# A 64-row second product for the attention scores, run over 128 rows with q low loaded twice

## The chip, the cores and the metric

The kernel runs on one core of one Trainium2 chip. The metric is the device time of one execution in microseconds (us); the median of three runs stands for a kernel. One further execution is recorded by the hardware profiler; its rows are what is read below. Engines: PE is TensorE's matmul side and PEld its weight load, DVE is VectorE, ACT ScalarE, POOL GpSimd, SP the queue that issues the DMAs.

## What is computed

One layer of a streaming encoder over 1072 token rows (32 sample rows, 16 learned meta rows, 1024 prompt rows): a mixer of three head groups (forgetting attention, multi-scale pooling, a chunked state-space scan), an output projection, and a dense gated FFN. The change touches the attention alone, six heads of 64:

```
s = einsum('bqhd,bkhd->bhqk', q, k) * HD_FOX ** -0.5
s = s + c_q[..., :, None] - c_k[..., None, :]          # cumulative log-forget bias
p = softmax(where(k_pos <= q_pos, s, -inf))
out = einsum('bhqk,bkhd->bqhd', p, v)
```

The prompt part is causal over 1040 rows; the 32 sample rows see 256 cached keys and their own.

## The kernel before, in words

All arithmetic is float32 to the outside. For TensorE every operand is split into a high part that the fast float32 format holds exactly and a low part, the rest; a product of two split operands is then three passes (high by high, high by low, low by high). `mm` (line 69) records every such product, so that nearly all of them carry line 69 and are told apart by the tile they write.

The program runs in stages: the input projection and the scan (to about 240 us), the attention (240 to 472 us), the output projection with its norms (to about 560 us) and the FFN (the rest). In the attention stage the order on each engine is written out by hand: the `while` loop of line 1124 runs in ticks. A tick issues, where they are due, one chunk of scores (`s_products`, line 995), one group of transposes of finished exponentials (`t_turn`, tiles `t`), the products with v (`o_products`, tiles `o`), the vector and scalar work that belongs to earlier ticks, and then filler: products of the next projections (`wk`) while there are any, later those of the output projection's first part (`wp`). How much filler follows is worked out from a planner's clock with a fixed estimate of TensorE's time (2 products by their columns, 100 ns on top, line 1141), and a head's scores are issued once the planner's clock has passed the estimated arrival of its loads (line 1138).

A head's operands lie in one tile `H`, of which there are two (`HA`, `HB`), filled by `prep(h)` (line 839) with DMAs from copies in HBM: K has k high in partitions 0 to 63 and k low in 64 to 127, Q has q high twice, QL has q low in partitions 0 to 63, bc the bias row, V and Vm the values. `arrival` (line 475) adds each DMA's bytes to the planner's estimate.

A chunk of scores takes up to 512 keys for up to 128 queries. It is one accumulation of two or three products: q high twice by K over 128 rows (which is high by high plus high by low in one pass), a mask product `identr` by `am` on the diagonal, and last q low by k high over 64 rows (line 1019). DVE then adds the bias and finds the row minimum (line 1029), ACT exponentiates (line 1040), PE transposes. There are 15 chunks in a head: four of 512 keys without a mask; one of 16, 144, 272, 400 or 512 keys with a mask two times each; and one of 304 keys for the 48 first queries, whose mask product has 48 rows. Six heads make 90 chunks.

Of the kernel before, what the change touches and what calls it, by code (L numbers as in the profile page):

```python
# [15 lines left out]
P = 128  # L16
D = 1024
NK = 8
NT = 1072
# [3 lines left out]
KEYS = PAST + NT  # L23
# [27 lines left out]
def tile_hybrid_trunk(ctx: ExitStack, tc: tile.TileContext, a: dict):  # L51
# [16 lines left out]
    def mm(out, lhsT, rhs, start, stop):  # L68
        return nc.tensor.matmul(out, lhsT, rhs, start=start, stop=stop, skip_group_check=True)  # L69
# [28 lines left out]
    def psum(tag, name):  # L98
        return where.get(tag, psp[0]).tile([P, 512], F32, tag=tag, bufs=PSB[tag], name=name)
# [14 lines left out]
    qd = [dr.tile([2, P, NT], F32, name=f"qd{p}") for p in range(3)]  # L114
# [7 lines left out]
    cd = dr.tile([6, KEYS], F32, name="cd")  # L122
# [110 lines left out]
    for t in range(9):  # L233
        R, o = TROW[t], TOFF[t]
# [4 lines left out]
        ps = zps[t]  # L239
# [98 lines left out]
    def cv_tile(tag, name):  # L338
        return CV.tile([P, EW], F32, tag=tag, bufs={"ext": 2, "cv": 4}[tag], name=name)
# [53 lines left out]
    for b in range(3):  # L393
        c0, n = CH[b]
        ps = psum("sm", f"ft{b}")
        for t in CTILES[b]:
            R, c = TROW[t], TOFF[t] - c0
# [47 lines left out]
    for i in range(5):  # L445
# [9 lines left out]
        h = cv_tile("cv", f"ch{i}")[:, :W]  # L455
# [19 lines left out]
    def arrival(nbytes):  # L475
        queue[0] = max(queue[0], clock[0]) + nbytes / 330.0
        return queue[0] + LATE[0]
# [333 lines left out]
    live, n = [], 0  # L811
# [27 lines left out]
    def prep(h):  # L839
        pr, hb = h // 2, 64 * (h % 2)  # L840
        H = (HB if h % 2 else HA).tile([P, HW], F32R, tag="H", name=f"H{h}")

        K, Q, QL = H[:, :KEYS], H[:, KEYS:KEYS + NT], H[:64, KEYS + NT:KEYS + 2 * NT]
        bc = H[:, KEYS + 2 * NT:2 * KEYS + 2 * NT]
        V = H[:, 2 * KEYS + 2 * NT:HW - P].rearrange("p (t c) -> p t c", c=P)
        Vm = H[:, HW - P:]
        heads[h] = (Q, QL, K, V, Vm, bc)
        v = vd[pr][:, h % 2].rearrange("r d j -> r (d j)")
        hs = slice(hb, hb + 64)
        loads = [(K[:64], kd[pr][0, hs]), (Q[:64], qd[pr][0, hs]), (K[64:], kd[pr][1, hs]), (Q[64:], qd[pr][0, hs]),  # L850
                 (QL, qd[pr][1, hs]), (bc, cd[h].partition_broadcast(P)),
                 (V[:, 0:2], v[0:PAST].rearrange("(t p) c -> p t c", p=P)), (V[:48, 2], v[PAST:PAST + 48]),
                 (Vm, v[PAST + 48 - P:PAST + 48]),
                 (V[:, 3:], v[PAST + 48:].rearrange("(t p) c -> p t c", p=P))]
        for i, (dst, src) in enumerate(loads):
            sync.dma_start(dst.bitcast(F32), src)
            at = arrival(4 * P * (KEYS if i == 5 else NT if i == 9 else KEYS // 2))
            if i % 2:
                yield
        ready[h] = at  # L860
# [113 lines left out]
    def geom(t):  # L974

        return TROW[t], TOFF[t], (0 if t == 0 else PAST + NS), (304 if t == 0 else NM + P * t)
# [13 lines left out]
    def place(t):  # L990

        free = [i for i in ring if SW[i] >= PAD + geom(t)[3]]
        return free[-1] if free else None

    def s_products(h, u, t, j, nch):
        Q, QL, K, V, Vm, bc = heads[h]
        R, o, k0, Lk = geom(t)
        if j == 0:
            st = AT.tile([P, 4], F32, tag="st", bufs=6, name=f"st{h}_{t}")
            i = place(t)  # L1000
            ring.remove(i)
            tiles[h, t] = (Sring[i], st)
            slot[h, t] = i
            if t in (0, 1, 3, 5, 7):
                i = 2 * ((5 * h + u) % 4)
                rows[h, u] = rsum[:, i:i + 2]
        j0 = 512 * j
        n = min(512, Lk - j0)
        ps = psum("s", f"s{h}_{t}_{j}")
        ks = slice(k0 + j0, k0 + j0 + n)  # L1010
        mm(ps[:R, :n], Q[:, o:o + R], K[:, ks], True, False)
        if t == 0:
            mm(ps[:R, :n], identr[:R, :R], am0, False, False)
        else:
            d0 = max(Lk - P, j0)
            d1 = j0 + n
            if d1 > d0:
                mm(ps[:R, d0 - j0:d1 - j0], identr, am[:, d0 - (Lk - P):d1 - (Lk - P)], False, False)
        mm(ps[:R, :n], QL[:, o:o + R], K[:64, ks], False, True)
        return ps  # L1020

    def s_min(h, u, t, j, nch, ps):
# [86 lines left out]
    def o_out(h, u):  # L1109
# [5 lines left out]
        outs.append((h, u))  # L1115

    side.append(prep(0))
    prepped = 0
    si = ti = n = 0
# [4 lines left out]
    while ti < len(Tgroups) or tolo or toprod or toout or later:  # L1124
# [11 lines left out]
        if si < len(Schunks):  # L1136
            c = Schunks[si]
            if (c[3] or place(c[2]) is not None) and clock[0] >= ready.get(c[0], 1e12):
                s = (c, s_products(*c))
                si += 1  # L1140
                work += 2 * min(512, geom(c[2])[3] - 512 * c[3]) / 2.4 + 100
# [14 lines left out]
        if tv:  # L1156
            for hi, lo, v in tv[1]:
                hi_of(hi, v)
            h, u, g, ng = tv[0]
# [8 lines left out]
        if s:  # L1168
            s_min(*s[0], s[1])
            h, u, t, j, nch = s[0]  # L1170
# [18 lines left out]
        if prepped < 5 and headsdone >= prepped and si > 3:  # L1189
            if prepped % 2 == 0 or len(filler) <= 2 - (prepped + 1) // 2 or (Schunks[si][0] == prepped  # L1190
                                                                           and Schunks[si][1] >= 4):
                if prepped % 2:
                    finish_qkv((prepped + 1) // 2)
                prepped += 1
                side.append(prep(prepped))
                if prepped == 5:
                    late_pool(0)
                    late_pool(1)
                    rawq += [late_attn(1, *c) for c in OCH]
# [242 lines left out]
    at = {"prep": 0, "raw": 0, "load": 0}  # L1442
# [59 lines left out]
    def prep_more(most=2):  # L1502
        while True:

            if at["prep"] >= items.index(("wd", 0, 1)) - 1:
                while at["load"] < min(at["raw"] + 3, len(wd_tiles)):
                    load_wd(*wd_tiles[at["load"]])
                    at["load"] += 1
            if at["prep"] == len(items) or not places or most == 0:
                break  # L1510
            prep()
            most -= 1
# [51 lines left out]
    for t in range(9):  # L1564
        ks = (3, 4) if t < 2 else (0, 1, 2, 3, 4)
# [547 lines left out]
```

## Time and profile before

| what | value |
|---|---|
| time, median of 3 runs | 1263.66 us (1263.57 to 1264.64) |
| the profiled execution: its own time | 1267.12 us |
| its span, first to last instruction | 1265.3 us |
| PE busy | 1224.8 us, 97% of the span |
| PEld busy | 1146.1 us, 91% |
| DVE busy | 843.5 us, 67% |
| ACT busy | 501.0 us, 40% |
| mean granted TensorE clock | 0.988 of full speed |

Busy times are sums over one engine's instructions. A matmul's recorded duration holds pipeline latency, and neighbours overlap, so the pace of a stream of products is read from one start to the next and not from the durations.

### The profile page before, as it was taken

What the parts mean: (1) busy time and instruction counts of PE and PEld (TensorE: products, weight loads), DVE (VectorE), ACT (ScalarE), POOL (GpSimd) and SP (SyncE); (2) the same over time, 40 slices, a digit from 0 to 9 for tenths busy, and PEclk for the clock granted to TensorE, in tenths of its full rate; (3) what the DMA queues carried; (4) which work ended last, traced back from release to release, by engine and by line L of the source; (5) the groups of instructions that cost most, each with busy time, mean ns of one, the idle gap of its engine ahead of it and who ended that gap; (6) DMA issues with size and microseconds to landing.
All of it is one profiled execution on the core that took longest, in us unless ns stands there. A gap on an engine that the chain in (4) does not pass through costs nothing.

```text
span 1265.3 us, 22956 instructions
## 1 busy us (share of the span) xinstructions
PE 1224.8 (97%) x8780; PEld 1146.1 (91%) x8780; DVE 843.5 (67%) x1620; ACT 501.0 (40%) x1104; POOL 193.2 (15%) x303
## 2 busy tenths in 40 slices
PE   7999899999999999889899999999999999999997
PEld 6999888888877776679899999999999999999996
DVE  4488687267676455675877777777777767555576
ACT  7422254245466562552432323223232335444432
POOL 0100386200122342440000000000000000000022
PEclk9999999999989999998999999999999999999998
DMA  9421264766665836551243444344433578655544
GB/s 299 148 82 55 63 175 151 243 199 182 200 193 174 262 109 229 201 168 67 77 137 138 171 145 162 133 151 154 167 128 137 196 273 302 243 187 181 186 145 148
DMA packets 128478, 213.85 MB, mean 169 GB/s; under 512 B 16227, under 2 KB 82857, under 8 KB 128369
## 3 DMA queue, kind: packets, MB, share of 16 engines
q1 hardware_dynamic: 123056, 191.57, 47.0%
q0 software_dynamic: 5312, 20.82, 4.3%
q8 instruction: 69, 1.13, 0.4%
q14 instruction: 41, 0.33, 0.1%
HBM read 144.66 MB, written 67.69 MB: 168 GB/s over the span
## 4 chain that ended last, share of the span: by engine, by line
PE 49%; DVE 1%; DMA 0%; issue 0%; ACT 0%; DVEq 0%; ACTq 0%
PE dn L69 14%; PE gy L69 14%; PE gz L69 9%; PE gx L69 9%; PE dl L69 3%; PE eT L1801 0%; DMA wsd<-ws 0%; DVE H L1367 0%; DVE ey L1831 0%; DVE HD L1367 0%; PE eT L1814 0%; DVE ey L1816 0%; DVE m L1663 0%; DVE T L1367 0%; DVE HT L1693 0%
## 5 line engine op out<-in xcount | busy, mean ns | idle before, releaser
L69 PE MATMUL wk<-T,wkh 128*128 128x384 f32 (+1 forms) x1152 | 205.2, 330 | 1.5 <-POOL wkh L66 0.8
L69 PEld LDWEIGHTS wk<-T,wkh 128*128 128x128 f32 x1152 | 186.8, 189 | 4.8 <-POOL wkh L66 1.1
L69 PE MATMUL gx<-T,HD 128*128 128x272 f32 (+1 forms) x960 | 120.5, 285 | 2.3 <-ACT m L1642 2.3
L69 PEld LDWEIGHTS gx<-T,HD 128*128 128x128 f32 x960 | 118.4, 188 | 2.5 <-ACT m L1642 2.5
L69 PE MATMUL gy<-H,HD 128*128 128x272 f32 (+1 forms) x960 | 119.3, 283 | 1.4 <-DVE m L1663 1.4
L69 PEld LDWEIGHTS gy<-H,HD 128*128 128x128 f32 x960 | 117.4, 188 | 1.6 <-DVE m L1663 1.6
L1367 DVE TENSOR_TENSOR HD<-rg,HD 128x512 fp32r<-128x512 f32 x126 | 86.1, 685 | 39.3 <-ACT HD L58 39.3
L69 PE MATMUL dn<-T,HD 128*128 128x272 f32 (+1 forms) x816 | 101.0, 285 | 0.4 <-DVE m L1663 0.4
L69 PEld LDWEIGHTS dn<-T,HD 128*128 128x128 f32 x816 | 100.1, 188 | 0.7 <-DVE m L1663 0.6
L69 PE MATMUL dn<-T,W 128*128 128x272 f32 (+1 forms) x768 | 94.7, 284 | 0.2 <-DVE W L1367 0.2
L69 PEld LDWEIGHTS dn<-T,W 128*128 128x128 f32 x768 | 93.9, 188 | 0.4 <-DVE W L1367 0.4
L1663 DVE TENSOR_TENSOR m<-gy,m 128x272 f32<-128x272 f32 x120 | 51.8, 432 | 48.8 <-PE gy L69 47.5
L58 ACT ACTIVATE HD<-rg 128x512 fp32r<-128x512 f32 x126 | 74.5, 624 | 18.5 <-PE gy L69 17.8
L58 ACT ACTIVATE PT<-t 128x512 fp32r<-128x512 f32 (+2 forms) x96 | 44.7, 472 | 90.1 <-PE t L1075 35.4
L1699 POOL DMA_DIRECT2D actd<-HT x20 | 15.3, 766 | 391.7 <-DVE HT L1675 273.8
L58 ACT ACTIVATE HD<-scr 128x512 fp32r<-128x512 f32 x20 | 12.7, 636 | 154.3 <-DVE scr L1498 154.3
L63 DVE TENSOR_TENSOR PT<-t,PT 128x512 fp32r<-128x512 f32 (+2 forms) x96 | 50.1, 527 | 31.9 <-ACT PT L58 31.0
L69 PE MATMUL s<-H 64*128 64x512 f32 (+5 forms) x180 | 65.0, 373 | 0.0
L69 PE MATMUL gy<-T,HD 128*128 128x272 f32 (+1 forms) x480 | 61.8, 285 | 0.0
L69 PE MATMUL gz<-T,HD 128*128 128x272 f32 (+1 forms) x480 | 61.6, 284 | 0.0
L69 PE MATMUL gz<-H,HD 128*128 128x272 f32 (+1 forms) x480 | 61.2, 283 | 0.0
L1367 DVE TENSOR_TENSOR T<-HT,T 128x528 fp32r<-128x528 f32 (+2 forms) x83 | 57.9, 704 | 4.9 <-ACT T L58 4.9
(309 smaller groups left out, 2276.3 us busy)
## 6 DMA issues: line engine op xcount, KB each, us to landing
rg<-in_wgu_dram SPq DMA_DIRECT2D x44, 512.0 KB
HT<-actd SPq DMA_DIRECT2D x77, 264.0 KB
actd<-HT POOLq DMA_DIRECT2D x11, 1056.0 KB, 5.7
ws<-in_wd_dram SPq DMA_DIRECT2D x44, 256.0 KB
wsd<-ws SPq DMA_DIRECT2D x44, 256.0 KB
rd<-wsd SPq DMA_DIRECT2D x20, 512.0 KB
wkr<-in_wx_dram SPq DMA_DIRECT2D x16, 512.0 KB
actd<-HT POOLq DMA_DIRECT2D x10, 792.0 KB, 4.0
```

Of the source, the lines that this page charges most:

```text
L58: nc.scalar.activation(out, in_, AF.Copy)
L63: nc.vector.tensor_tensor(out=out, in0=in_, in1=hi.bitcast(F32), op=ALU.subtract)
L69: return nc.tensor.matmul(out, lhsT, rhs, start=start, stop=stop, skip_group_check=True)
L1367: (eng or dv).tensor_tensor(out=lo, in0=raw, in1=hi.bitcast(F32), op=SUB)
L1663: return lambda h, ps: dv.tensor_tensor(out=out[:, PART[h]], in0=ps, in1=other[:, PART[h]], op=ADD)
L1699: nc.gpsimd.dma_start(actd[r0:r0 + n, :, p].rearrange("s p n -> p s n"), HT[:, 2 * (p % 2) + 1 - q, CHN * s0:CHN * (s0 + n)].rearrange("p ...
```

## The change

Partitions 64 to 127 of QL, until now unused, get a second copy of q low by one more DMA (64 partitions by 1072 columns, 268 KB) in each head. The second product then runs over all 128 rows: q low by k high plus q low by k low. The count of products and their columns stay as they are; the low by low term is added to the sum. Two indices in `prep`'s planner account move by one place since the list of loads has one more entry.

```
-        K, Q, QL = H[:, :KEYS], H[:, KEYS:KEYS + NT], H[:64, KEYS + NT:KEYS + 2 * NT]
+        K, Q, QL = H[:, :KEYS], H[:, KEYS:KEYS + NT], H[:, KEYS + NT:KEYS + 2 * NT]
...
-                 (QL, qd[pr][1, hs]), (bc, cd[h].partition_broadcast(P)),
+                 (QL[:64], qd[pr][1, hs]), (QL[64:], qd[pr][1, hs]), (bc, cd[h].partition_broadcast(P)),
...
-            at = arrival(4 * P * (KEYS if i == 5 else NT if i == 9 else KEYS // 2))
+            at = arrival(4 * P * (KEYS if i == 6 else NT if i == 10 else KEYS // 2))
...
-        mm(ps[:R, :n], QL[:, o:o + R], K[:64, ks], False, True)
+        mm(ps[:R, :n], QL[:, o:o + R], K[:, ks], False, True)
```

Since the planner counts one more load, its clock lets a head start a little later, and the written order shifts through the whole attention stage. Three places show how.

On SP, head 0's loads (tile `H`; `kd`, `qd`, `cd`, `vd` are the copies of k, q, bias and v in HBM, `wkr` the raw weights of a projection). Before:

```order
L856 DMA H_2404<-kd_73 64x1328
L856 DMA H_2404<-qd_70 64x1072
L856 DMA H_2404<-kd_73 64x1328
L856 DMA H_2404<-qd_70 64x1072 x2
L856 DMA H_2404<-cd 128x1328
L627 DMA wkr_2431<-in_wx_dram 128x1024
```

After:

```order
L856 DMA H_2404<-kd_73 64x1328
L856 DMA H_2404<-qd_70 64x1072
L856 DMA H_2404<-kd_73 64x1328
L856 DMA H_2404<-qd_70 64x1072 x3
L627 DMA wkr_2431<-in_wx_dram 128x1024
L856 DMA H_2404<-cd 128x1328
```

The second q-low load stands behind the first, and the projection's weights have moved ahead of the bias row.

On PE, the entry into the attention (`wk` are projection products, `s_0_0` the first chunk of scores, `s_1_0` the second). Before:

```order
L69 MATMUL wk_688_2504<-T,wkh_2291 128x384 x24
L69 MATMUL wk_0_2540<-T,wkh_2499 128x304 x9
L69 MATMUL s_0_0_2551<-H_2404 48x304
L69 MATMUL s_0_0_2551<-am_98,identr 48x304
L69 MATMUL s_0_0_2551<-H_2404 48x304
L69 MATMUL wk_0_2540<-T,wkh_2499 128x304 x15
```

After:

```order
L69 MATMUL wk_688_2505<-T,wkh_2291 128x384 x24
L69 MATMUL wk_0_2538<-T,wkh_2500 128x304 x24
L69 MATMUL wk_304_2578<-T,wkh_2500 128x384 x3
L69 MATMUL s_0_0_2583<-H_2404 48x304
L69 MATMUL s_0_0_2583<-am_98,identr 48x304
L69 MATMUL s_0_0_2583<-H_2404 48x304
L69 MATMUL wk_304_2578<-T,wkh_2500 128x384 x15
```

Eighteen projection products (15 of 304 columns, 3 of 384) have moved ahead of the first chunk of scores; the filler between later chunks is thinner by as many.

On SP, the first of head 1's loads and what stands ahead of them (`vd`, `out_o_vT`, `kp` belong to the projections, `rd` and `od` to head 0's results). Before:

```order
L583 DMA out_o_vT_dram<-v_304_2652 128x384
L856 DMA H_2693<-kd_73 64x1328
L856 DMA H_2693<-qd_70 64x1072
L856 DMA H_2693<-kd_73 64x1328
L856 DMA H_2693<-qd_70 64x1072 x2
L856 DMA H_2693<-cd 128x1328
```

After:

```order
L583 DMA out_o_vT_dram<-v_304_2648 128x384
L554 DMA vd_77<-vhl_0_2674 48x256
L554 DMA vd_77<-vhl_0_2674 128x2x256
L627 DMA wkr_2704<-in_wx_dram 128x1024
L554 DMA vd_77<-vhl_304_2697 128x3x256
L583 DMA out_o_vT_dram<-v_688_2702 128x384
L597 DMA kp_2739<-in_cache_kT_dram 128x256
L856 DMA H_2741<-kd_73 64x1328
L856 DMA H_2741<-qd_70 64x1072
```

Six transfers of the projections that stood behind or between head 1's loads now stand ahead of them.

## Rows read from the trace of the kernel before

**Rows 1.** The page's first part: busy us, share of the span, instructions.

```profile
PE 1224.8 (97%) x8780; PEld 1146.1 (91%) x8780; DVE 843.5 (67%) x1620; ACT 501.0 (40%) x1104; POOL 193.2 (15%) x303
```

**Rows 2.** Waits of PE, 238 to 480 us: line, releaser, us, times, longest.

```profile
PE t L1063 <- DVE T L63: 1.0, 1, 1.0
PE wk L69 <- POOL wkh L66: 0.8, 1, 0.8
```

**Rows 3.** Windows: length, busy us of PE, PEld, DVE, ACT, POOL, clock, DMA share, GB/s.

```profile
240.00:472.00 232.00, 229.49 (x1374) 188.16 (x1373) 146.54 (x362) 125.17 (x317) 50.49 (x53) 0.99 0.63 188
345.00:365.00 20.00, 18.24 (x121) 14.29 (x120) 17.29 (x44) 14.51 (x37) 3.21 (x3) 0.99 0.51 172
364.60:371.40 6.80, 6.80 (x26) 5.32 (x26) 5.27 (x15) 3.07 (x9) 4.59 (x4) 0.50 0.81 212
...
400.00:424.00 24.00, 24.00 (x135) 18.69 (x135) 14.02 (x35) 13.48 (x31) 3.98 (x6) 1.00 1.01 294
```

**Rows 4.** PE by line and shape, 238 to 470 us: busy us, mean ns.

```profile
L69 PE MATMUL s<-H 64*128 64x512 f32 x36 | 18.1, 504 | 0.0
L69 PE MATMUL s<-H 128*128 128x512 f32 x36 | 14.9, 413 | 0.0
```

**Rows 5.** Timeline of PE, merged: start us, length us, operation, count (404 to 408.8 us).

```profile
404.18 0.85 PE L69 MATMUL wp<-wo,T 128*128 128x512 f32 x3
404.87 0.23 PE L69 MATMUL s<-H 128*128 128x144 f32 x1
...
405.39 0.66 PE L1075 MATMUL t<-ident,S 128*128 128x128 f32 x4
...
406.81 0.83 PE L69 MATMUL s<-H 128*128 128x512 f32 x2
407.57 0.66 PE L1075 MATMUL t<-ident,S 128*128 128x128 f32 x4
407.99 0.94 PE L69 MATMUL wp<-wo,T 128*128 128x512 f32 x3
```

**Rows 6.** The same timeline: transposes between 128-row products, and the other chunk shapes.

```profile
378.07 0.34 PE L69 MATMUL s<-H 128*128 128x400 f32 x1
...
378.77 0.66 PE L1075 MATMUL t<-ident,S 128*128 128x128 f32 x4
...
384.16 0.17 PE L69 MATMUL s<-H 128*128 128x16 f32 x1
...
384.57 0.33 PE L1075 MATMUL t<-ident,S 128*128 128x128 f32 x1
...
389.18 0.60 PE L1075 MATMUL t<-ident,S 128*128 128x128 f32 x4
389.53 1.65 PE L69 MATMUL wp<-wo,T 128*128 128x512 f32 x6
391.01 0.30 PE L69 MATMUL s<-H 128*48 128x304 f32 x1
...
391.66 0.66 PE L1075 MATMUL t<-ident,S 128*128 128x128 f32 x4
...
398.36 0.39 PE L69 MATMUL s<-H 128*128 128x512 f32 x1
...
399.15 0.66 PE L1075 MATMUL t<-ident,S 128*128 128x128 f32 x4
...
408.76 0.29 PE L69 MATMUL s<-H 128*128 128x272 f32 x1
...
409.36 0.33 PE L1075 MATMUL t<-ident,S 128*128 128x128 f32 x1
```

**Rows 7.** Timeline of SP (issue) and PE (use): head 5's bias load and first scores.

```profile
415.23 0.58 SPq L856 DMA_DIRECT2D H<-cd  x1
433.65 0.30 PE L69 MATMUL s<-H 128*48 128x304 f32 x1
```

## The prediction

> **What bounds the kernel now.** I read the page's first part, the waits of PE, the windows of the stage that the change touches, and then the timeline of PE. PE is busy for 97% of the span [rows 1]. In the attention stage PE is busy for 229.49 of 232.00 us, DVE for 146.54, ACT for 125.17, and the DMA engines for 0.63 of the time [rows 3]. In that stage PE waits five times, 0.6 to 1.0 us each; the longest is on DVE, the next on the weights that POOL prepares [rows 2]. So what PE no longer has to do there comes off the end, until DVE or ACT become late. The narrowest place is 345 to 365 us: DVE is busy for 17.29 of 20.00 us, PE for 18.24 [rows 3]. After the waits of that stretch the granted clock fell to 0.50, that is to 1.2 of 2.4 GHz, from 364.6 to 371.4 us [rows 3].
>
> **What a 64-row product costs.** Its durations say little, since neighbours overlap; I read from start to start. Three `wp` products of 512 columns over 128 rows take 404.87 - 404.18 = 0.69 us, or 0.23 each [rows 5]. Two score products of 512 columns, one over 128 rows and one over 64, take 407.57 - 406.81 = 0.76 us to the start of the transposes behind them [rows 5], where two at 0.23 would take 0.46. So 0.30 us is lost between entry and exit. The transposes behind also start late: four of them take 407.99 - 407.57 = 0.42 us behind a 64-row product [rows 5] and 389.53 - 389.18 = 0.35 behind a 128-row one [rows 6]. That is 0.07; I take 0.06, since two rounded differences stand in it. So an unmasked chunk loses 0.36 us at the passage from 128 rows to 64 and back.
>
> The Trainium skill (TensorEngine Tiling (Array Packing), Key Properties) says that changing the tiling mode drains TensorE, which is what these rows look like; the trace agrees, with 0.36 us for one way out and back.
>
> **What the change removes.** For the masked chunks I do the same sum. A 128-row product of n columns is put at 0.23 x n / 512 us (0.18 for 400, 0.14 for 304, 0.12 for 272), and at 0.11 us at least, since four transposes in a row take 0.35 us with the last one overlapped by its successor [rows 6]. The mask product in the middle is at that floor, but for the 48-row one. From the first product's start to the start of what follows:
> - 144 keys: 405.39 - 404.87 = 0.52 now [rows 5], three at the floor 0.33 then: 0.19 saved.
> - 272 keys: 409.36 - 408.76 = 0.60 now [rows 6], 0.12 + 0.11 + 0.12 = 0.35 then: 0.25.
> - 400 keys: 378.77 - 378.07 = 0.70 now [rows 6], 0.18 + 0.11 + 0.18 = 0.47 then: 0.23.
> - 512 keys with a mask: 399.15 - 398.36 = 0.79 now [rows 6], 0.23 + 0.11 + 0.23 = 0.57 then: 0.22.
> - 16 keys: 384.57 - 384.16 = 0.41 now [rows 6], 0.33 then: 0.08.
> - 304 keys, 48 queries: 391.66 - 391.01 = 0.65 now [rows 6]. Here the mask product itself has 48 rows, so the passage stays and moves to it: two products of 304 columns that each pay a passage (0.14 plus about 0.09) and one that doesn't, 0.60: 0.05 saved.
>
> Counts: 24 chunks of the unmasked kind, 12 of each of the five masked kinds, 6 of 48 queries. The sum is 24 x 0.30 = 7.2, plus 12 x (0.19 + 0.25 + 0.23 + 0.22 + 0.08) = 11.6, plus 6 x 0.05 = 0.3, plus the late start of what follows, 84 x 0.06 = 5.0 (the 48-query chunks keep theirs): **24.1 us** of PE.
>
> No row shows a second score product over 128 rows, so the sum has two bounds. The small one takes the recorded durations alone: 504 ns over 64 rows against 413 over 128 at 512 columns [rows 4], 0.09 us in each of 90 products, 8.2 us. The large one adds that with fewer late steps the half clock of 364.6 to 371.4 us does not come (6.8 us at half speed, 3.4 us) and that the two waits for projection weights go (1.5 us, with the 0.8 of [rows 2] the longer): 29 us. I take 24.1, since the 0.23 and 0.35 us that stand in it are measured on the same engine with the same operand types, a few products away.
>
> **What it adds and moves.** One DMA of 268 KB for each head, 1.6 MB in six. At the 294 GB/s of the fullest stretch [rows 3] that is 0.9 us of DMA time per head. Head 5's bias load is issued at 415.23 us and its first scores run at 433.65 us [rows 7], so 18 us cover it: nothing on the path. The issue costs SP about half a microsecond, and only result stores and loads are queued behind. For head 0 the projection's raw weights now stand ahead of the bias load; the two waits for prepared weights can only get shorter, at most by the 1.5 us above. I count nothing.
>
> The written order moves 18 projection products ahead of the first scores: 15 x 0.14 + 3 x 0.17 = 2.6 us. PE does them anyway, so that costs nothing unless the filler is missed later, where it covers the chain from scores to minimum, exponential and transposes. Head 1's loads now stand behind six transfers of the projections, but its first scores have also moved back by the same planner's clock.
>
> **What becomes late next.** DVE and ACT keep their work while PE loses 24.1 of 232 us. Over the stage DVE would then be busy for 146.54 of 208 us, 70%: room on the average. In 345 to 365 us, PE would give up 11 products at 0.27 us (the 24.1 us over 90), 3.0 us, and DVE has 2.7 us free in all; I count half as lost, 1.5 us. For the other 79 products I allow 2 us of new waits, which is what the five waits of now come to within a factor of two, and 1 us for the filler that has moved to the front. That leaves 24.1 - 1.5 - 2 - 1 = **19.6 us**. The half clock of 364.6 us follows a wait in the DVE-bound stretch, and I leave it as it is.
>
> The profiled execution took 1267.12 us with a span of 1265.3; its span would fall to 1245.7. It is 3.5 us above the median, and I take the same 19.6 us from the median: 1263.66 - 19.6 = 1244.1, forecast as **1244 us**. What comes after 472 us starts earlier by the same time: its weights come by loads that follow PE's own progress.
>
> **The rivals.**
> - *The passage goes, but DVE and ACT set the ticks.* Each tick is a chain from scores to minimum to exponential to transposes, on three engines, and with 0.27 us less on PE it may surface. For it: DVE's 17.29 of 20 us, and the exponential and transposes only one tick apart. Against it: PE hardly waits today, and filler fills most ticks. Priced at 0.1 us of new wait in each of 90 chunks, 9 us, and one more fall of the clock like that at 364.6 us, 3.4 us: 24.1 - 12.4 = 11.7 gained, 1252 us.
> - *Nothing is gained, since weight loads aren't hidden.* If the 0.36 us were the uncovered weight load of the product and of its successor, it would stay, because both products use partitions 0 to 63 before and after: the time would be that of now, 1264 us. Against it: the three `wp` products at 0.23 us each load new weights every time and show no such loss [rows 5]. The Trainium skill (TensorE: Matmul & The Clock Gate, Part 3, The mechanism) states that a weight load overlaps running matmuls only where the row groups differ; by that rule this rival would hold, and the `wp` rows contradict it.
> - *Slower: the heads' loads come late.* A head's 11 loads can only start when the head two before it has freed its tile, and a shorter stage leaves them less time. If PE had to wait 5 us for each of six heads, with a fall of the clock once, it would lose 30 + 3.4 us and gain 24.1: 1263.7 + 9.3 = 1273 us. It decides from 4 us of wait per head. Against it: the 18 us of room in [rows 7], in the stretch where the DMA engines are fullest (1.01) [rows 3].
>
> **How the numbers follow.** Forecast (1238 to 1249 us) 0.75; ticks set by DVE and ACT (1249 to 1256) 0.16; nothing gained 0.05; slower 0.04. A measurement of this kernel tells about 0.2%, 2.5 us, from no change: the first two are faster by more, 0.91; the third is the same, 0.05; the last is slower, 0.04. The range: below, 24.1 us gained and a little of the half clock too, 1238; above, most of the first rival, 1254. About 0.13 lies outside.
>
> **What would show it.** In the trace after, `s` has 90 products over 128 rows where the 64-row ones were, two of 512 columns take 0.46 us from start to start with the successor, and four transposes behind them take 0.35. PE's waits in the stage stay under 6 us in all and DVE's share rises to about 70%. If the 0.76 us stays, the cost wasn't in the rows. If PE's waits on `PT` (DVE), `S` (ACT) rise to 10 us, the first rival holds. If PE waits for a DMA into `H`, the last one does. A stretch of half clock more or less moves the time by 3.4 us and would spoil the size, not the sign.

## The result: just under half of the forecast gain

| what | before | after |
|---|---|---|
| time, median of 6 runs each, same comparison | 1263.84 us (1262.39 to 1264.64) | 1253.64 us (1251.70 to 1260.02) |
| the profiled execution: its own time, span | 1267.12, 1265.3 us | 1252.72, 1250.9 us |

The ratio is 0.9926, with an interval from 0.9903 to 0.9948: 9.4 us gained, between 6.6 and 12.3. The forecast was 1244 us, a gain of 19.6. The sign held, and the time lies at the very edge of the range (1238 to 1254); more than half of the gain is missing.

The page of after, its span and its first part (busy us, share of the span, instructions), answers to [rows 1]:

```profile
span 1250.9 us, 22978 instructions
...
PE 1205.0 (96%) x8780; PEld 1145.3 (92%) x8780; DVE 840.9 (67%) x1620; ACT 500.2 (40%) x1104; POOL 194.7 (16%) x303
```

PE is busy for 19.8 us less, with as many instructions, and the span is 14.4 us shorter in this execution. The timeline of PE in after (start us, length us, operation, count) answers to [rows 5, 6]:

```profile
380.73 0.30 PE L69 MATMUL s<-H 128*48 128x304 f32 x1
...
381.41 0.60 PE L1075 MATMUL t<-ident,S 128*128 128x128 f32 x4
...
393.99 0.23 PE L69 MATMUL s<-H 128*128 128x144 f32 x1
...
394.28 0.62 PE L1075 MATMUL t<-ident,S 128*128 128x128 f32 x4
...
395.65 0.63 PE L69 MATMUL s<-H 128*128 128x512 f32 x2
396.11 0.60 PE L1075 MATMUL t<-ident,S 128*128 128x128 f32 x4
396.47 0.95 PE L69 MATMUL wp<-wo,T 128*128 128x512 f32 x3
397.25 0.29 PE L69 MATMUL s<-H 128*128 128x272 f32 x1
...
397.62 0.27 PE L1075 MATMUL t<-ident,S 128*128 128x128 f32 x1
...
400.63 0.34 PE L69 MATMUL s<-H 128*128 128x400 f32 x1
...
401.11 0.60 PE L1075 MATMUL t<-ident,S 128*128 128x128 f32 x4
...
403.38 0.40 PE L69 MATMUL s<-H 128*128 128x512 f32 x1
...
403.96 0.60 PE L1075 MATMUL t<-ident,S 128*128 128x128 f32 x4
...
404.87 0.17 PE L69 MATMUL s<-H 128*128 128x16 f32 x1
...
405.12 0.33 PE L1075 MATMUL t<-ident,S 128*128 128x128 f32 x1
```

Start to start, two score products of 512 columns take 396.11 - 395.65 = 0.46 us (forecast 0.46, before 0.76), and the four transposes behind them 396.47 - 396.11 = 0.36 (0.35). With a mask: 144 keys 0.29 (0.33), 272 keys 0.37 (0.35), 400 keys 0.48 (0.47), 512 keys 0.58 (0.57), 16 keys 0.25 (0.33). Only the 48-query chunks save nothing: 381.41 - 380.73 = 0.68 (0.60, before 0.65). By these starts the sum is 24 x 0.30 + 12 x (0.23 + 0.23 + 0.22 + 0.21 + 0.16) - 6 x 0.03 + 84 x 0.06 = 24.7 us, where the forecast had 24.1. The chunks shown are no exceptions: from the first product to what follows, all 90 chunks of the two timelines add up to 61.0 us in before and 41.6 in after, 19.4 us less without the last term. So PE's own work became as short as forecast.

The weight loads show where the time was lost. PEld in before, beside the two score products of [rows 5] (in brackets: idle time before):

```profile
407.14 0.18 PEld L69 LDWEIGHTS s<-H 64*128 64x128 f32 x1 [0.36 <-issue]
407.57 0.42 PEld L1075 LDWEIGHTS t<-ident,S 128*128 128x128 f32 x4 [0.25 <-issue]
```

PEld in after, beside the two at 395.65 us:

```profile
395.42 0.42 PEld L69 LDWEIGHTS s<-H 128*128 128x128 f32 x2
395.88 0.59 PEld L1075 LDWEIGHTS t<-ident,S 128*128 128x128 f32 x4
```

In before the transposes and their first weight load both start at 407.57 us. In after the load starts at 395.88 and the transposes at 396.11, so it lies beside the product ahead of it. At a change of the row count the weight load was not covered by the product before it; between equal row counts it is.

What the stage made of it stands in its waits and windows. In them `pp` is the SBUF tile into which ACT copies (evacuates) finished `wp` sums, `PT` holds transposed exponentials, and `ot` the results of the products with v. Waits of PE in after, 238 to 480 us (releaser, us in total, times, longest), against the five waits of [rows 2]:

```profile
PE wp L69 <- ACT pp L938: 3.9, 1, 3.9
PE o L69 <- ACT ot L1113: 2.0, 4, 0.8
PE o L69 <- DVE PT L63: 1.9, 3, 0.8
PE wk L69 <- DVE k L572: 1.2, 1, 1.2
```

Windows of after (length, busy us of PE, PEld, DVE, ACT, POOL, clock, DMA share, GB/s), against [rows 3]:

```profile
240.00:472.00 232.00, 220.73 (x1419) 193.78 (x1418) 147.56 (x367) 129.67 (x326) 53.50 (x55) 0.99 0.72 212
333.00:358.00 25.00, 20.90 (x148) 17.02 (x146) 20.98 (x52) 17.37 (x46) 3.33 (x3) 1.00 0.75 221
...
408.00:420.00 12.00, 9.00 (x58) 7.60 (x56) 2.90 (x5) 4.10 (x10) 2.28 (x3) 1.00 0.87 268
420.90:424.30 3.40, 3.40 (x9) 2.67 (x10) 1.09 (x2) 1.57 (x5) 2.85 (x4) 0.51 0.33 129
```

All waits of PE there come to 11.9 us, against 3.8 in before. In the DVE-bound stretch (333 to 358 us) DVE is busy for 20.98 of 25 us, but each wait is below 1 us. The new one is a single wait of 3.9 us, of the products `wp` on the evacuation `pp`, and most of it lies in 408 to 420 us, where PE is busy for 9.00 of 12 us and DVE and ACT for 2.90 and 4.10. Neither of them is the bound there; the DMA engines are the busiest, at 0.87 of the time. Half clock (0.51) follows the wait at 420.9 us.

The chain behind this wait takes three timelines. PE in after, where it waits (in brackets: idle time before, and releaser):

```profile
416.38 0.62 PE L69 MATMUL o<-PT,H 128*128 128x256 f32 x4
420.87 1.65 PE L69 MATMUL wp<-wo,T 128*128 128x512 f32 x3 [3.87 <-ACT pp L938]
```

ACT in after, its evacuations of `wp` into `pp`. Two of them fill one tile, and there are two tiles:

```profile
399.53 0.58 ACT L938 ACTIVATE pp<-wp 128x512 f32<-128x512 f32 x1
...
411.14 0.59 ACT L938 ACTIVATE pp<-wp 128x512 f32<-128x512 f32 x1
...
420.22 0.60 ACT L938 ACTIVATE pp<-wp 128x512 f32<-128x512 f32 x1 [5.60 <-DMA ppd<-pp]
```

SP in after, when it issues the last loads of head 5 and the stores of `pp`:

```profile
414.25 0.37 SPq L856 DMA_DIRECT2D H<-vd  x1
414.92 0.32 SPq L940 DMA_DIRECT2D ppd<-pp  x1
...
416.93 0.52 SPq L940 DMA_DIRECT2D ppd<-pp  x1
```

The first tile is full at 399.53 + 0.58 = 400.1 us, and its store is issued at 414.92, 14.8 us later, right behind the last of head 5's loads. The next evacuation into this tile has to wait for the store until 420.22, and PE for the evacuation. In before, the same store stands at the same place in SP's order, behind all loads of head 5. There ACT's rows are:

```profile
416.26 0.59 ACT L938 ACTIVATE pp<-wp 128x512 f32<-128x512 f32 x1
...
428.74 0.60 ACT L938 ACTIVATE pp<-wp 128x512 f32<-128x512 f32 x1 [0.67 <-DMA ppd<-pp]
```

SP's rows there:

```profile
422.36 1.43 SPq L856 DMA_DIRECT2D H<-vd  x2
...
424.36 0.33 SPq L940 DMA_DIRECT2D ppd<-pp  x1
```

There the tile is full at 416.85, its store leaves at 424.36, and ACT waits 0.67 us and PE not at all. So the evacuation now comes 16.7 us earlier (416.85 to 400.1), the store only 9.4 (424.36 to 414.92).

Why the store moved less is in the windows from the issue of the pooling's results `T<-pd` (L868, 2.1 MB, issued just ahead of head 5's loads) to that store. In before:

```profile
399.30:424.30 25.00, 25.00 (x143) 19.60 (x143) 14.72 (x35) 14.08 (x33) 4.68 (x7) 1.00 0.97 283
```

In after:

```profile
388.60:414.90 26.30, 25.73 (x165) 22.39 (x164) 16.12 (x38) 15.73 (x36) 5.72 (x8) 1.00 1.01 279
```

In both, the DMA engines are full from end to end (0.97 and 1.01). The stretch takes 25.0 us before and 26.3 after, although PE is faster. PE's work beside it became shorter, and PE came to need the `pp` tile again before its store had gone. Whether the DMA engines' work sets that length is tested by e4 and e10.

### The profile page after: what moved, and what is told of

The parts are those of the page before. It is cut to its first block, busy times and chain, and to the rows that moved or that the text cites. A ratio compares the mean times of both kernels' runs of the same rounds, so it can differ in the third digit from the quotient of the medians.

```text
span 1250.9 us, 22978 instructions
## 1 busy us (share of the span) xinstructions
PE 1205.0 (96%) x8780; PEld 1145.3 (92%) x8780; DVE 840.9 (67%) x1620; ACT 500.2 (40%) x1104; POOL 194.7 (16%) x303
## 4 chain that ended last, share of the span: by engine, by line
PE 79%; DVE 7%; DMA 6%; ACT 3%; POOL 2%; issue 2%; SPq 1%; DVEq 0%; ACTq 0%; POOLq 0%
PE dn L69 15%; PE gy L69 14%; PE wk L69 13%; PE gx L69 9%; PE gz L69 9%; PE dl L69 3%; PE s L69 2%; PE wp L69 2%; PE o L69 2%; PE z L69 2%; PE t L1075 2%; DVE cx L1292 1%; PE sy L69 1%; DMA or<-od 1%; PE wo L69 1%
## 5 line engine op out<-in xcount | busy, mean ns | idle before, releaser
L69 PE MATMUL o<-PT,H 128*128 128x256 f32 (+1 forms) x324 | 59.2, 297 | 4.2 <-ACT ot L1113 2.0
```

## The experiments

The runs e1 to e4, e5 to e8 and e9 to e11 form three groups, each taken beside runs of before, with medians of 1264.34, 1265.76 and 1265.62 us. The kernel after was not run again, so differences of 1 or 2 us between groups are no finding.

First question: is the missing half due to the extra load and the moved order, or to DVE and ACT?

**e1: the loads of after, the order of before.** The planner doesn't count the second load.

```
-                 (QL[:64], qd[pr][1, hs]), (QL[64:], qd[pr][1, hs]), (bc, ...),
+                 (QL[:64], qd[pr][1, hs]), (bc, ...),
...
+            if i == 4:
+                sync.dma_start(QL[64:].bitcast(F32), src)
```

> The 128-row second product and its extra load, but the planner doesn't count that load, so that the written order on every engine is that of the kernel before. Theory 1 (the shifted order costs the missing gain: it puts products of wp where their evacuation must wait for a store behind head 5's loads): the 3.9 us wait of wp on ACT pp is gone, time 1244 to 1248 us. Theory 2 (with 24 us less on PE the ticks of DVE and ACT and the DMA traffic set the pace in any order): waits of PE in the stage stay near 12 us, 1251 to 1256 us.

Measured: 1249.83 us, ratio 0.9884 (0.9865 to 0.9903), between the two expectations. PE still waits for `pp`, 2.5 us in place of 3.9.

**e2: the loads and order of after, the second product over 64 rows again.**

```
-        mm(ps[:R, :n], QL[:, o:o + R], K[:, ks], False, True)
+        mm(ps[:R, :n], QL[:64, o:o + R], K[:64, ks], False, True)
```

> The changed kernel's loads and written order, but the second product again over 64 rows (q low by k low is left out again, as in the kernel before). Theory 1 (order): the order costs 6 to 10 us by itself, so this one is slower than the kernel before, 1268 to 1274 us. Theory 2 (the ticks): order and load cost nothing as long as PE is slow, 1262 to 1266 us.

Measured: 1268.73 us, ratio 1.0042 (1.0021 to 1.0063). Loads and order by themselves cost 4 to 5 us (by the interval 3 to 8). There is no wait for `pp` here, and the profiled execution (1266.96 us) is no longer than that of before (1267.12), so the profile doesn't show where this cost lies. Between e2 and after lie 1.2%, 15 us: that is what the rows alone bring, given the same loads and order.

**e3: no extra load.** The order of before; the second product takes Q, which is in SBUF over 128 rows, in place of QL.

```
-        mm(ps[:R, :n], QL[:, o:o + R], K[:, ks], False, True)
+        mm(ps[:R, :n], Q[:, o:o + R], K[:, ks], False, True)
```

> The written order and the loads of the kernel before, and a second product over 128 rows that takes q high again in place of q low (so q low is left out of the scores and the outputs aren't the reference's): the passage between row counts goes without the extra 268 KB per head. If the extra load is what the DMA queue can't take: 4 to 6 us faster than the run with the order of before. If the load is hidden: the same time as that one within 2 us. By the sum of the prediction, PE's own work falls by 24 us in either.

Measured: 1246.59 us, ratio 0.9864 (0.9841 to 0.9887). The wait for `pp` is down to 1.5 us. By the medians the load costs some 3 us against e1 (the intervals overlap), between the two expectations, though no score product waits for it.

**e4: the 2.1 MB of `T<-pd` issued later**, after head 4 is done and not ahead of head 5's loads; all else as in after.

```
                 if prepped == 5:
-                    late_pool(0)
-                    late_pool(1)
...
             HX = HA.tile(...)
+            late_pool(0)
+            late_pool(1)
```

> The changed kernel, with the 2.1 MB load of the pooling part into T moved from ahead of head 5's loads to after head 4's last product. If the store of the partial products is late because the DMA queue is full between 390 and 420 us: the wait of wp on ACT pp falls from 3.9 us to under 1 us and the fall of the clock behind it goes, 5 to 6 us faster than the changed kernel, 1247 to 1249 us. If ACT or the order sets that wait: it stays, 1252 to 1255 us.

Measured: 1245.01 us, ratio 0.9854 (0.9834 to 0.9873), 8.6 us better than after. The wait for `pp` is gone, and the time is below what was expected. The window of e4 from head 5's first load to the store:

```profile
388.88:406.90 18.02, 17.45 (x113) 15.26 (x113) 13.11 (x34) 11.93 (x29) 5.70 (x8) 1.00 1.02 264
```

Without the 2.1 MB the stretch is 8.3 us shorter (26.3 to 18.0) with the DMA engines as full as before (1.02), and the store leaves at 406.89 in place of 414.92. So it is mostly the bytes to be moved that set its length.

**e5: e1 and e4 together.** **e6: only e4's move, in the kernel of before** (64 rows, no extra load).

> Both remedies: the order of the kernel before (the extra load is made but not counted) and the pooling load into T moved behind head 4. If the store of the partial products behind a full DMA queue is what ate the gain in both orders (2.5 us of wait still stood in the run with the order of before): the wait of wp on ACT pp is gone, 1242 to 1245 us. If the two remedies cure the same thing in part, no faster than the run with the pooling load moved alone: 1245 to 1247 us.

> The kernel before, 64 rows, with nothing but the pooling load moved. Theory: as long as PE is slow the DMA queue is no bound, and the move gains nothing, 1261 to 1266 us. Rival: the load's place was a cost of its own all along, and the 8 to 9 us that moving it gained in the changed kernel come here too, 1254 to 1257 us.

Measured: e5 1245.05 us, ratio 0.9839 (0.9820 to 0.9858), the same as e4 alone, so the two cure the same loss. e6 1264.43 us, ratio 0.9987 (0.9970 to 1.0004): nothing gained. The late store is no loss to the kernel of before; it became one when PE became faster.

Second question: is it the place of the store in SP's order, or the full DMA engines as such?

**e9: after, with one line changed: the store is issued from ACT's queue.**

```
-                sync.dma_start(ppd[TOFF[t]:TOFF[t] + TROW[t]], st[:TROW[t]])
+                nc.scalar.dma_start(ppd[TOFF[t]:TOFF[t] + TROW[t]], st[:TROW[t]])
```

> The changed kernel, with the stores of the partial products issued from ACT's queue and not behind the head loads on SP's. In the changed kernel the store came 3.2 us after its data were ready (SP) and landed 5.3 us after that. If SP's order is what delays it: the wait of wp on ACT pp falls by 3 us or goes, 1247 to 1250 us. If the DMA engines are full whatever the queue: the wait stays within 1.5 us of 3.9, 1252 to 1255 us.

Measured: 1245.24 us, ratio 0.9846 (0.9817 to 0.9874), 8.4 us better than after (some 10 by the ratios), and better than expected. The 3.2 us in the expectation pairs the store with a later evacuation; the right figure for after is the 14.8 us above. ACT in e9:

```profile
399.51 0.33 ACTq L940 DMA_DIRECT2D ppd<-pp  x1
...
410.36 0.59 ACT L938 ACTIVATE pp<-wp 128x512 f32<-128x512 f32 x1
410.98 0.33 ACTq L940 DMA_DIRECT2D ppd<-pp  x1
...
413.73 0.60 ACT L938 ACTIVATE pp<-wp 128x512 f32<-128x512 f32 x1
```

and the window of e9 against that of after above:

```profile
408.00:420.00 12.00, 12.00 (x73) 10.29 (x72) 3.85 (x6) 6.87 (x15) 5.57 (x8) 1.00 0.99 299
```

Each store follows its evacuation at once. The one that left at 414.92 in after leaves at 399.51, the next evacuation into its tile runs at 413.73 with no wait, and PE is busy for all of 12 us, while the DMA engines are as full as ever (0.99). So full DMA engines alone don't make PE wait; the store's place in SP's queue behind them does. The Trainium skill (DMA: Bandwidth & Descriptors, Issuing engines are not separate DMA queues) states that starting DMAs from several engines only saves the time of issuing them, usually little beside the DMA itself. Here SP's order held a store back by 14.8 us, and another queue was worth 8.4 us; the measurement decides.

**e10: after, with the second load replaced by a memset of zeros on POOL** (the product is then that of before, padded to 128 rows).

```
+            if i == 5:
+                nc.gpsimd.memset(dst.bitcast(F32), 0.0)
+            else:
                 sync.dma_start(dst.bitcast(F32), src)
```

> The changed kernel in its own planned order, but the lower 64 partitions of QL are set to zero by GpSimd and not loaded (1.6 MB of DMA less). If the extra load is what tips the full queue: the wait of wp on ACT pp falls to under 1.5 us, 1246 to 1249 us. If the load is a small part of it (0.9 us of DMA time per head): the wait falls by about 1 us, 1251 to 1253 us.

Measured: 1250.41 us, ratio 0.9890 (0.9862 to 0.9918), between the two expectations, though the wait is as short as the first of them has it. The wait in e10:

```profile
PE wp L69 <- ACT pp L941: 0.9, 1, 0.9
```

The window of e10 from `T<-pd` to the store:

```profile
389.22:412.80 23.58, 23.01 (x148) 20.03 (x148) 15.18 (x36) 14.08 (x33) 5.24 (x7) 1.00 1.00 300
```

Without its 268 KB the stretch takes 23.6 us in place of 26.3, and the wait is 3.0 us shorter: the load lengthens the stretch by about as much as PE waits more. By the medians the load alone is worth 3.2 us of the 8.4 (e10 against after, overlapping intervals), the moved order alone 3.8 (e1), and both together 7.0 (e3). So load and order are what made the store too late for PE, each in part, and the store's place (e9) or the 2.1 MB ahead of it (e4) are where it can be cured with both left in.

Third question: is the passage between row counts really what was saved, and is more of it to be had?

**e7: e5 with the memset in place of the load.** **e8: e5 with the 48-row mask product padded to 128 rows.**

```
-    am0 = WH.tile([48, 304], F32R, name="am0")
+    am0 = WH.tile([P, 304], F32R, name="am0")
...
-    nc.scalar.activation(am0, amr[:48, P:], AF.Copy)
+    nc.scalar.activation(am0, amr[:, P:], AF.Copy)
...
-            mm(ps[:R, :n], identr[:R, :R], am0, False, False)
+            mm(ps[:R, :n], identr[:, :R], am0, False, False)
```

> As the run with both remedies, but the lower 64 partitions of QL are set to zero by GpSimd (one memset of 64 by 1072 per head) and not loaded: 128 rows without the 1.6 MB of DMA. If the extra load still costs: 1.5 to 4 us faster than that run, as q high in place of q low was against the order of before (3.2 us). If the full queue was all that the load cost: the same within 1.5 us, or slower where GpSimd's queue is held up by the memset waiting for a free tile.

> As the run with both remedies, and the mask product of the first chunk of each head runs over 128 rows (48 real ones and zeros) where it ran over 48, between two products over 128. If the passage between row counts is what costs: the three products of 304 columns take 0.42 us from the first start to the start behind them where they took 0.68, 1.5 us less over six heads; in the time that is hardly to be seen (0 to 3 us less). If the weight load or the second writing of a PSUM bank is what costs: the starts don't change.

Measured: e7 1243.82 us, ratio 0.9819 (0.9791 to 0.9847); with the store out of the way the load costs some 1 us by the medians, and the intervals of e5 and e7 overlap, so that no cost of it is shown. e8 1242.93 us, ratio 0.9821 (0.9802 to 0.9840), overlapping e5's too; what decides is the timeline of PE. The 304-column chunk in e5:

```profile
379.48 0.30 PE L69 MATMUL s<-H 128*48 128x304 f32 x1
379.71 0.34 PE L69 MATMUL s<-am,identr 48*48 48x304 f32 x1
379.98 0.35 PE L69 MATMUL s<-H 128*48 128x304 f32 x1
380.16 0.60 PE L1077 MATMUL t<-ident,S 128*128 128x128 f32 x4
```

The same chunk in e8:

```profile
379.25 0.30 PE L69 MATMUL s<-H 128*48 128x304 f32 x1
379.39 0.30 PE L69 MATMUL s<-am,identr 128*48 128x304 f32 x1
379.53 0.30 PE L69 MATMUL s<-H 128*48 128x304 f32 x1
379.67 0.60 PE L1077 MATMUL t<-ident,S 128*128 128x128 f32 x4
```

Three products of the same columns take 0.68 us with a 48-row one in the middle and 0.42 with none. The passage costs 0.26 us here, where only the mask product's row count changed: the row count, and no special trait of the 64-row operand, is what costs.

**e11: all that helped**: the order of before, `T<-pd` later, the mask over 128 rows, zeros by memset.

> Everything that helped at once: order of before, pooling load moved, mask product over 128 rows, q low's second copy replaced by a memset. If the gains add: 1 us below the run with the mask over 128 rows and 2 us below the one with the memset, 1241 to 1243 us.

Measured: 1239.76 us, ratio 0.9805 (0.9779 to 0.9831), the lowest median of all, a little below what was expected, and 14 us below after. Its interval overlaps those of e7 and e8, so what the pieces add to each other isn't shown. Whether a third `pp` tile would do the same as e9 wasn't tried.

## Why the prediction was half right

- **PE bounds the stage: right.** With the store out of the way (e9) the work taken from PE came off the end. The stage's last `o` product starts at 471.49 us in before, 460.54 in after, 454.60 in e9.
- **The passage and its size: right.** 24.7 us by after's own starts for 24.1; the sums over all chunks agree; e8 shows the same cost in another product. The single terms are within 0.04 us but for the 16-key chunk (0.25 for 0.33) and the 48-query one (0.68 for 0.60).
- **What it adds and moves, priced at nothing: wrong, and the step that failed.** The 18 us of room [rows 7] were head 5's own, and no score product did wait for a load. But room was only counted for whoever uses the loaded data. The sentence "only result stores and loads are queued behind" named the victim and put no price on it: a store in that queue frees one of two `pp` tiles, and PE's filler needs the tile. The row that speaks of it was there, the DMA share of 1.01 from 400 to 424 us [rows 3]: work of the DMA engines that doesn't shrink while PE's does. The term was put at 0. Load and moved order measure 7.0 us together (e3 against after), and the late store through which they act 8.4 us (e9 against after). The profiled executions of after and e9 are 7.5 us apart (1250.9 and 1243.4), and 5.9 of it lie within the stage (460.54 - 454.60): 3.9 us of wait, by estimate 1.7 for the half clock of 420.9 to 424.3 us, and 0.3 that no row names. Nor does a row account for the 1.6 us after the stage.
- **What becomes late next, 4.5 us for DVE, ACT and filler: about right.** With the store cured, after and the order of before both come to 1245 us (e9, e5), a gain of 19 to 20 us by the ratios, where 19.6 was forecast. PE's waits in the stage come to 8.3 us in e9 against 3.8 in before, 4.5 more: 1.7 in the DVE-bound stretch (forecast 1.5) and 2.8 elsewhere (3). The sign that was named, under 6 us of waits in all, didn't fit this sum and failed, with 11.9 us in after and 8.3 in e9.
- **First rival (DVE and ACT set the ticks, 1252 us): near in time, wrong in mechanism.** Its rows would be waits on `PT` and `S` of 10 us; they come to 1.9 and 0.6. The long wait was on `pp`, and behind ACT's evacuation stood a DMA.
- **Second rival (nothing gained): refuted as told, but near in cause.** Two products over 128 rows take 0.46 us with new weights for each, so the cost doesn't stay. The rows of PEld above do show an uncovered weight load at the passage; it goes with the change of the row count, and the use of partitions 0 to 63 doesn't keep it.
- **Third rival (heads' loads late): refuted as told**, since PE waits nowhere for a DMA into `H`. It had the right resource, the DMA engines at 1.01, and the wrong party.
- **What stays open:** the 4 to 5 us that loads and order cost in e2, with no wait for `pp`, and the 1.6 us after the stage. That e10 gained only 3 us fits the moved order that it keeps (e1), by medians alone.

## What to carry to other kernels

When work is taken from the bounding engine, go through the stretches where the DMA engines are full: their length follows the bytes (25.0 and 26.3 us here), and the engine arrives earlier at whatever stands at their end. For each transfer that is added to an in-order queue, price not only the reader of its data but each store queued behind it, by the buffers that the store frees and the time until they are needed next. And where, as here, a product over 64 or 48 rows stands between products over 128, padding it with a copy or with zeros is worth a try: 0.26 to 0.36 us for each.

## What was not expected of the hardware

A product of fewer rows costs mostly by the passage in and out and little by its own columns: 0.30 us at 512 columns, 0.22 and 0.23 us at 400 and 144 columns with a mask product between, and 0.26 us for three products of 304 columns. At the passage the weight load is not covered (the transposes' load starts with them at 407.57 us in before, 0.23 us ahead of them in after). That stores of 512 KB, issued from ACT's queue with the DMA engines at 0.99, are done in time, while on SP one of them was issued 14.8 us late, shows that the place in a queue can cost what full DMA engines alone do not.
